# Decoder step on one core: cache tiles loaded from the Pool queue into three buffers, dilated queries kept in token order, one rotary table

## The chip, the cores and the metric

The kernel runs on one core of a Trainium2 chip. The metric is the device time of one execution in microseconds (us). A core has TensorE (PE; its weight loads are listed apart as PEld), VectorE (DVE), ScalarE (ACT), GpSimd (POOL) and SyncE (SP, which here only issues DMAs). Engines run their own instruction streams in order and meet through semaphores. "SPq" is the issuing side of SP.

## The reference, cut to what matters

Two layers of a decoder trunk are computed for 1024 prompt tokens and for a sample group of 8 sequences with 4 new tokens each. The first layer is gated linear attention, the second a dilated attention over one shared K/V. Both are followed by a SwiGLU and a gated embedding. What the change touches is the second layer's attention:

```python
DIL_GROUPS = ((128, 1), (512, 4), (2048, 16))
q = (h @ w_q).reshape(B, L, N_GROUPS, N_KV, Q_PER_KV, HEAD_DIM)   # 3 groups, 4 kv heads x 2, 128
q = rope_partial(rms_norm(q, q_norm), pos)
for g, (win, dil) in enumerate(DIL_GROUPS):
    o, l = attend(q[:, :, g], win, dil)     # prompt: a band of win/dil keys of the same class mod dil
    ...                                     # sample: the same keys, gathered from cache_k/cache_v + new ones
w = jax.nn.softmax(jnp.stack(lses), axis=0)
o = jnp.sum(w[..., None] * jnp.stack(outs), axis=0)
```

The sample tokens read `cache_k` and `cache_v`, of which the host lays out the 640 rows that any of the three groups can reach, per head and per half (four sequences) as five tiles of 128 x 512.

## The kernel before, in words

Tokens are columns: T = 1056 = 1024 prompt tokens (NP) and 32 sample tokens, cut into three chunks of CW = 352. Activations live as 128 x 1056 tiles, features on the partitions. Every large product is done as three products of rounded parts (`hi*hi`, `hi*lo`, `lo*hi`), each weight 128 x 128 against 352 columns. The program is traced in Python with a framework that sets all semaphores and that also sets the order on each engine's queue, from priorities and its own estimates of when things come due; a change of one operation can so move others.

The second layer's attention is the class `Mixer`, driven by `mixer`. There are eight head slots. For slot `s`, `queries(s)` makes three query tiles (one for each dilation group) from `XH`, `XL` (L949, 72 matmuls of 352 columns each tile), normalizes each with `qk_head` and turns the first 32 features by a rotary table. `attend(s, q)` then does the prompt attention, and after every second slot `sample(h, half)` is called twice for the sample tokens of that kv head. Products of the next slot's queries (L949) are woven between the small matmuls of `attend` and `sample`.

In `qk_head`, `finish` writes `q * g * rstd` into the query tile (L817). For the groups 1 and 2 (`classes=True`) it writes in class order instead: column `r*256 + u` holds token `4u + r` (L821), with a separate small instruction for the sample tokens of the last chunk (L825). The rotary table for those two groups is a second one in class order (`c_rope[1]`). `rotate` (L829 to L832) is the same for all. `sample_part` copies the sample columns of each query tile to `Qs` on POOL (L956).

In `attend`, group 0 is matched against `KA` (keys in token order, L985); the groups 1 and 2 against `KB` (the same keys in class order, copied by POOL at L933), with the queries of class `r` and half `h` as the stationary operand (L996): a contiguous run of 128 columns. Each of these matmuls is issued as two passes with a weight load each. The keys are 128 columns wide for `h = 0` and 256 for `h = 1`.

In `sample`, five key tiles `kk` (128 x 512, L1091) and five value tiles `vv` (L1136) are loaded by SP into two buffers each; eight small matmuls read each tile (L1095, L1139), after which its buffer is free. SP also issues, in the same queue, the query weights (`raw`, L260), `KA`, `VB`, `VA` (L931 to L939), the small round trips through DRAM for softmax statistics (`scr`, `stX`, `cA`, L989 to L1019) and the results.

Of the kernel before, what the change touches and what calls it, by code (L numbers as in the profile page):

```python
# [19 lines left out]
T = NP + NS  # L20
# [15 lines left out]
def yoco_step_kernel(  # L36
# [768 lines left out]
    def qk_head(chunks, g, tab, tp, dst, pre, late, classes=False, early=False):  # L805
# [4 lines left out]
        def finish(s, q, t, th, tl):  # L810
            p = sm.pools[0].tile([128, CW], F32, tag="sm", name="p_n")
            nc.tensor.matmul(p, ones_r, th, start=True, stop=False)
            nc.tensor.matmul(p, ones_r, tl, start=False, stop=True)
            nc.scalar.activation(t, p, AF.Ln, scale=1.0 / 128, bias=epsb)
            nc.scalar.activation(t, t, AF.Exp, scale=-0.5)
            if not classes:
                nc.vector.scalar_tensor_tensor(dst[:, s], q, g, t, op0=ALU.mult, op1=ALU.mult)  # L817
                return
            e = min(s.stop, NP) - s.start
            u = slice(s.start // 4, (s.start + e) // 4)  # L820
            nc.vector.scalar_tensor_tensor(  # L821
                dst[:, :NP].rearrange("p (r u) -> p u r", r=4)[:, u], q[:, :e].rearrange("p (u r) -> p u r", r=4), g,
                t[:, :e].rearrange("p (u r) -> p u r", r=4), op0=ALU.mult, op1=ALU.mult)
            if e < CW:
                nc.vector.scalar_tensor_tensor(dst[:, NP:], q[:, e:], g, t[:, e:], op0=ALU.mult, op1=ALU.mult)  # L825
# [23 lines left out]
    def rope_table(pool, i=0):  # L849
        tab = pool.tile([64, T], F32, name=f"tab{i}")  # L850
        nc.sync.dma_start(tab, c_rope[i])
# [46 lines left out]
    class Mixer:  # L898
        def __init__(self, st, mq):
# [14 lines left out]
            self.tab = [rope_table(p, i) for i in range(2)]  # L914
# [37 lines left out]
        def queries(self, s):  # L952
# [7 lines left out]
            for g in range(3):  # L960
                q = self.pool.tile([128, T], F32, tag="q", name="q", bufs=QB)
                flush = qk_head(self.proj(wtile(w_q[3 * s + g]), XH, XL), gcol(G_Q), self.tab[g > 0], self.pool, q,
                                self.pre, late, classes=g > 0)
# [5 lines left out]
        def attend(self, slot, q):  # L969
# [20 lines left out]
            for r in range(4):  # L990
                for h in range(2):
                    n = 128 * (h + 1)
                    s = slice(r * 256 + 128 * h, r * 256 + 128 * h + 128)
# [87 lines left out]
        def sample(self, h, half):  # L1081
# [8 lines left out]
            for a in range(5):  # L1090
                kk = sp.tile([128, 512], F32, tag="kk", name="kk", bufs=2)  # L1091
                nc.sync.dma_start(kk, ck[h, half, a])
# [42 lines left out]
            for a in range(5):  # L1135
                vv = sp.tile([128, 512], F32, tag="vv", name="vv", bufs=2)  # L1136
                nc.sync.dma_start(vv, cv[h, half, a])
# [211 lines left out]
```

## Time and profile before

| | us |
|---|---|
| median of three runs | 2946.8 (2945.55 to 2947.34) |
| the profiled execution, whole | 2945.02 |
| its span, first to last instruction | 2943.2 |
| TensorE busy in the span | 2891.9 (98%) |
| VectorE / ScalarE / GpSimd busy | 1851.8 / 1087.5 / 19.8 |
| mean granted TensorE clock | 0.996 |

The two feed-forward blocks keep TensorE busy without a break. The attention of the second layer lies between about 1440 and 2060 us of the span. The profile gives for each engine its busy time, for each group of instructions a count, busy time and mean, and for idle time what ended it.

### The profile page before, as it was taken

How to read it: one execution, taken by the hardware profiler on the slowest of the kernel's cores; microseconds unless marked ns; L12 is line 12 of the kernel's file. 1: busy time of each engine (PE TensorE's matmuls, PEld its weight loads, DVE VectorE, ACT ScalarE, POOL GpSimd, SP SyncE). 2: the span in 40 equal slices, each digit the busy share in tenths (PEclk: the TensorE clock that was granted, in tenths of full speed). 3: DMA queues.
4: the chain of work that ended last, by engine and by line, in shares of the span. 5: the costliest groups of instructions: out<-in, count | busy, mean ns of one | idle time of the engine just before them, and what ended most of it. 6: DMA issues, size and time to landing. Idle time of an engine off the chain costs nothing.

```text
span 2943.2 us, 47238 instructions
## 1 busy us (share of the span) xinstructions
PE 2891.9 (98%) x19920; PEld 2757.5 (94%) x19920; DVE 1851.8 (63%) x2781; ACT 1087.5 (37%) x1769; POOL 19.8 (1%) x44
## 2 busy tenths in 40 slices
PE   8999999999999999999999999989999999999999
PEld 7999898999999999999988888878899999999999
DVE  6444465776666544568587778774676666653474
ACT  5333344422222221235455555552532222231141
POOL 0000000000000000000000000000000000000000
PEclk9999999999999999999999999999999999999999
DMA  3121244222222532142523141334422222262123
GB/s 130 59 74 51 74 145 162 105 88 73 81 82 72 198 115 67 47 141 88 152 73 109 52 124 44 116 116 133 162 81 73 88 73 81 77 235 77 51 80 111
DMA packets 134419, 291.07 MB, mean 99 GB/s; under 512 B 34592, under 2 KB 59168, under 8 KB 133184
## 3 DMA queue, kind: packets, MB, share of 16 engines
q1 hardware_dynamic: 133040, 287.72, 29.7%
q8 instruction: 157, 2.57, 0.4%
q10 hardware_dynamic: 1168, 0.34, 0.1%
q14 instruction: 54, 0.44, 0.0%
HBM read 216.15 MB, written 71.86 MB: 98 GB/s over the span
## 4 chain that ended last, share of the span: by engine, by line
PE 89%; DVE 5%; DMA 3%; ACT 2%; issue 1%; SPq 0%; DVEq 0%; ACTq 0%
PE mm L271 39%; PE be L207 13%; PE ga L207 9%; PE al L207 9%; PE mm L949 6%; PE mm L681 2%; PE p_s L996 1%; PE mm L289 1%; DMA vv<-in_cv_dram 1%; PE p_o L1064 1%; PE p_s L985 1%; DVE q L821 1%; DVE hs L829 1%; PE p_u L505 1%; PE p_o L514 1%
## 5 line engine op out<-in xcount | busy, mean ns | idle before, releaser
L134 ACT CAST whi<-raw 128x1024 fp32r<-128x1024 f32 (+2 forms) x244 | 197.6, 810 | 774.6 <-PE mm L271 562.0
L776 DVE TENSOR_TENSOR X<-mm,X 128x1056 f32<-128x1056 f32 (+1 forms) x100 | 120.8, 1212 | 238.2 <-PE mm L271 238.1
L135 DVE TENSOR_TENSOR wlo<-raw,whi 128x1024 fp32r<-128x1024 f32 (+2 forms) x244 | 224.3, 919 | 72.0 <-ACT whi L134 71.9
L271 PE MATMUL mm<-XH,whi 128*128 128x352 f32 x1104 | 250.8, 331 | 0.4 <-ACT q_in L295 0.4
L271 PE MATMUL mm<-XH,wlo 128*128 128x352 f32 x1104 | 247.2, 328 | 0.0
L271 PE MATMUL mm<-XL,whi 128*128 128x352 f32 x1104 | 244.9, 326 | 0.0
L134 ACT CAST hw<-S 128x512 fp32r<-128x512 f32 x176 | 108.9, 621 | 313.3 <-PE ga L207 181.6
L271 PE MATMUL mm<-GH,wlo 128*128 128x352 f32 x1038 | 223.5, 323 | 0.0
L271 PE MATMUL mm<-GL,whi 128*128 128x352 f32 x1038 | 223.5, 323 | 0.0
L271 PE MATMUL mm<-GH,whi 128*128 128x352 f32 x1038 | 223.1, 323 | 0.0
L207 PE MATMUL be<-Bh,hw 128*128 128x264 f32 x1056 | 215.9, 286 | 5.2 <-ACT hw L134 5.2
L207 PE MATMUL be<-Bl,hw 128*128 128x264 f32 x1056 | 215.0, 285 | 0.0
L207 PE MATMUL be<-Bh,lw 128*128 128x264 f32 x1056 | 214.3, 284 | 0.0
L271 PEld LDWEIGHTS mm<-XH,whi 128*128 128x128 f32 x1104 | 188.8, 189 | 7.6 <-ACT XH L137 1.7
L949 PE MATMUL mm<-XH,whi 128*128 128x352 f32 x576 | 193.9, 337 | 0.0
L949 PE MATMUL mm<-XL,whi 128*128 128x352 f32 x576 | 193.9, 337 | 0.0
L271 PEld LDWEIGHTS mm<-XL,whi 128*128 128x128 f32 x1104 | 189.5, 189 | 3.4 <-issue 2.7
L271 PEld LDWEIGHTS mm<-XH,wlo 128*128 128x128 f32 x1104 | 189.1, 189 | 2.7 <-issue 2.0
L949 PE MATMUL mm<-XH,wlo 128*128 128x352 f32 x576 | 189.6, 329 | 0.0
L271 PEld LDWEIGHTS mm<-GL,whi 128*128 128x128 f32 x1038 | 177.0, 188 | 0.3 <-DVE GL L135 0.2
L271 PEld LDWEIGHTS mm<-GH,whi 128*128 128x128 f32 x1038 | 176.5, 188 | 0.0
L271 PEld LDWEIGHTS mm<-GH,wlo 128*128 128x128 f32 x1038 | 176.5, 189 | 0.0
(346 smaller groups left out, 6281.8 us busy)
## 6 DMA issues: line engine op xcount, KB each, us to landing
raw<-in_w_fi_dram SPq DMA_DIRECT2D x88, 512.0 KB, 3.5
Gd<-g SPq DMA_DIRECT2D x44, 528.0 KB, 2.7
gr<-Gd SPq DMA_DIRECT2D x44, 528.0 KB, 4.9
raw<-in_w_fo_dram SPq DMA_DIRECT2D x64, 256.0 KB, 2.7
raw<-in_w_a_dram SPq DMA_DIRECT2D x24, 512.0 KB, 3.5
raw<-in_w_q_dram SPq DMA_DIRECT2D x24, 512.0 KB, 3.6
kk<-in_ck_dram SPq DMA_DIRECT2D x40, 256.0 KB, 3.1
vv<-in_cv_dram SPq DMA_DIRECT2D x40, 256.0 KB, 3.0
```

The source lines that it names most:

```text
L134: nc.scalar.copy(hi, x)
L135: nc.vector.tensor_tensor(lo, x, hi.bitcast(F32), op=ALU.subtract)
L207: nc.tensor.matmul(ps[:, c, :HC], a[:, k, :], b[:, c * HC:(c + 1) * HC], start=(first and k == 0 and i == 0), stop=(k == len(xs) - 1 and i ...
L271: nc.tensor.matmul(ps[:, c, :CW], a[:, k, :], b[k][:, c * CW:(c + 1) * CW], start=(k == 0 and i == 0), stop=(k == n - 1 and i == 2),)
L289: nc.tensor.matmul(ps, a[:, k, :], b[k][:, s], start=(k == 0 and i == 0), stop=(k == n - 1 and i == 2))
L505: nc.tensor.matmul(p, kr[:, j], vt[:, j], start=True, stop=True)
L514: nc.tensor.matmul(po[:, i], vt[:, j, v], atts[j // 4][:, j % 4], start=True, stop=(j == 0))
L681: nc.tensor.matmul(ps[:, c, :CW], raw[:, 128 * k:128 * k + 128], ps_[k][:, c * CW:(c + 1) * CW], start=(k == 0), stop=(k == 1))
L776: nc.vector.tensor_tensor(like(X[m], s, p), p, like(X[m], s, p), op=ALU.add)
L821: nc.vector.scalar_tensor_tensor(dst[:, :NP].rearrange("p (r u) -> p u r", r=4)[:, u], q[:, :e].rearrange("p (u r) -> p u r", r=4), g, t[: ...
L829: nc.vector.stream_shuffle(t[32:64], dst[:32], [(a + 16) % 32 for a in range(32)])
L949: nc.tensor.matmul(ps, a[:, k, :], b[k][:, s], start=(k == 0 and i == 0), stop=(k == n - 1 and i == 2))
```

## The change

There are three edits. The query tiles of the groups 1 and 2 are written in token order like those of group 0, so `qk_head` loses its `classes` branch (L819 to L825) and the mixer its second rotary table; `attend` then takes the queries of a class as every fourth column of the query tile (L993). The key and value cache tiles are loaded by a DMA issued from the POOL queue. Each of the two has three buffers.

```diff
--- before.py
+++ after.py
@@ -802,7 +802,7 @@
         return tc.keep_in_program_order(nc.scalar.preload_act_table_set("natural_log_exp_and_others"))
 
 
-    def qk_head(chunks, g, tab, tp, dst, pre, late, classes=False, early=False):
+    def qk_head(chunks, g, tab, tp, dst, pre, late, early=False):
         def flush():
             while late:
                 late.pop(0)()
@@ -813,16 +813,7 @@
             nc.tensor.matmul(p, ones_r, tl, start=False, stop=True)
             nc.scalar.activation(t, p, AF.Ln, scale=1.0 / 128, bias=epsb)
             nc.scalar.activation(t, t, AF.Exp, scale=-0.5)
-            if not classes:
-                nc.vector.scalar_tensor_tensor(dst[:, s], q, g, t, op0=ALU.mult, op1=ALU.mult)
-                return
-            e = min(s.stop, NP) - s.start
-            u = slice(s.start // 4, (s.start + e) // 4)
-            nc.vector.scalar_tensor_tensor(
-                dst[:, :NP].rearrange("p (r u) -> p u r", r=4)[:, u], q[:, :e].rearrange("p (u r) -> p u r", r=4), g,
-                t[:, :e].rearrange("p (u r) -> p u r", r=4), op0=ALU.mult, op1=ALU.mult)
-            if e < CW:
-                nc.vector.scalar_tensor_tensor(dst[:, NP:], q[:, e:], g, t[:, e:], op0=ALU.mult, op1=ALU.mult)
+            nc.vector.scalar_tensor_tensor(dst[:, s], q, g, t, op0=ALU.mult, op1=ALU.mult)
 
         def rotate():
             t = tp.tile([64, T], F32, tag="hs", name="hs")
@@ -846,9 +837,9 @@
         late.append(rotate)
         return flush
 
-    def rope_table(pool, i=0):
-        tab = pool.tile([64, T], F32, name=f"tab{i}")
-        nc.sync.dma_start(tab, c_rope[i])
+    def rope_table(pool):
+        tab = pool.tile([64, T], F32, name="tab")
+        nc.sync.dma_start(tab, c_rope[0])
         return tab
 
 
@@ -911,7 +902,7 @@
             self.Qs = [p.tile([128, 8, 32], F32, name=f"Qs{h}") for h in range(4)]
             self.kn = p.tile([128, 4, 32], F32, name="kn")
             self.os = p.tile([128, 8, 8, 4], F32, name="os")
-            self.tab = [rope_table(p, i) for i in range(2)]
+            self.tab = rope_table(p)
             self.head(0)
             self.pre = ln_exp_set()
             for h in range(4):
@@ -959,8 +950,8 @@
 
             for g in range(3):
                 q = self.pool.tile([128, T], F32, tag="q", name="q", bufs=QB)
-                flush = qk_head(self.proj(wtile(w_q[3 * s + g]), XH, XL), gcol(G_Q), self.tab[g > 0], self.pool, q,
-                                self.pre, late, classes=g > 0)
+                flush = qk_head(self.proj(wtile(w_q[3 * s + g]), XH, XL), gcol(G_Q), self.tab, self.pool, q,
+                                self.pre, late)
                 late.append(lambda g=g, q=q: sample_part(g, q))
                 out.append(q)
             flush()
@@ -990,7 +981,7 @@
             for r in range(4):
                 for h in range(2):
                     n = 128 * (h + 1)
-                    s = slice(r * 256 + 128 * h, r * 256 + 128 * h + 128)
+                    s = slice(512 * h + r, 512 * h + 512, 4)
                     ps = sc.tile([128, 2 * n], F32, tag="sc", name="p_s")
                     for g in range(2):
                         nc.tensor.matmul(ps[:, g * n:g * n + n], q[1 + g][:, s], self.KB[:, r * 256:r * 256 + n],
@@ -1088,8 +1079,8 @@
             s0 = sc.tile([128, 512], F32, tag="sc", name="p_ss")
             s1 = sc.tile([128, 144], F32, tag="sc", name="p_ss")
             for a in range(5):
-                kk = sp.tile([128, 512], F32, tag="kk", name="kk", bufs=2)
-                nc.sync.dma_start(kk, ck[h, half, a])
+                kk = sp.tile([128, 512], F32, tag="kk", name="kk", bufs=3)
+                nc.gpsimd.dma_start(kk, ck[h, half, a])
                 out = s0[:, a * 128:(a + 1) * 128] if a < 4 else s1[:, :128]
                 for q, b, rs in quads():
                     nc.tensor.matmul(out[rs], Qs[:, b], kk[:, q * 128:(q + 1) * 128], start=True, stop=True,
@@ -1133,8 +1124,8 @@
             nc.scalar.copy(pt[:16, 5], p[:16, 1])
             po = self.po.tile([128, 128], F32, tag="sm", name="p_os")
             for a in range(5):
-                vv = sp.tile([128, 512], F32, tag="vv", name="vv", bufs=2)
-                nc.sync.dma_start(vv, cv[h, half, a])
+                vv = sp.tile([128, 512], F32, tag="vv", name="vv", bufs=3)
+                nc.gpsimd.dma_start(vv, cv[h, half, a])
                 for q, b, rs in quads():
                     nc.tensor.matmul(po[rs], pt[:, a, rs], vv[:, q * 128:(q + 1) * 128], start=(a == 0), stop=False,
                                      tile_position=(0, 32 * q))
```

## Rows read from the trace of the kernel before

**Rows 1.** The page's part 1: busy us (share of span) xinstructions of each engine.
```profile
PE 2891.9 (98%) x19920; PEld 2757.5 (94%) x19920; DVE 1851.8 (63%) x2781; ACT 1087.5 (37%) x1769; POOL 19.8 (1%) x44
```

**Rows 2.** Busy us by window: length, PE, PEld, DVE, ACT, POOL, PEclk, DMA share, GB/s.
```profile
1440.00:2060.00 620.00, 591.41 (x4043) 523.64 (x4042) 456.63 (x1100) 319.91 (x745) 17.08 (x32) 0.99 0.33 98
600.00:700.00 100.00, 100.00 (x821) 100.00 (x820) 68.86 (x94) 28.05 (x40) 0.00 (x0) 1.00 0.24 80
1600.00:1610.00 10.00, 8.21 (x81) 6.98 (x80) 8.33 (x22) 4.14 (x11) 0.72 (x1) 0.89 0.70 241
1610.00:1620.00 10.00, 9.47 (x78) 7.80 (x78) 4.45 (x9) 3.70 (x9) 0.00 (x0) 0.94 0.35 104
```

**Rows 3.** Waits of PE, 1440 to 2060 us: who for whom, total, times, longest.
```profile
PE p_os L1139 <- DMA vv<-in_cv_dram: 4.6, 7, 1.8
PE p_s L985 <- DVE stA L978: 3.1, 7, 0.9
PE mm L949 <- DVE OL L135: 3.0, 2, 2.7
PE p_t L1053 <- DVE pA L1050: 2.9, 3, 1.8
PE p_ss L1095 <- DMA kk<-in_ck_dram: 2.7, 4, 1.3
```

**Rows 4.** Timeline of SP's issues from 1600 us: start, us, what.
```profile
1600.61 1.18 SPq L1137 DMA_DIRECT2D vv<-in_cv_dram  x2
...
1606.89 5.69 SPq L1137 DMA_DIRECT2D vv<-in_cv_dram  x3
```

**Rows 5.** Timeline of PE from 1606 us: start, us, what, idle time before and releaser.
```profile
1606.40 0.43 PE L1139 MATMUL p_os<-vv,pts 128*32 128x128 f32 x8 [1.79 <-DMA vv<-in_cv_dram]
...
1608.57 0.49 PE L949 MATMUL mm<-XL,whi 128*128 128x352 f32 x1
```

**Rows 6.** DMA issues, 1440 to 2060 us: what, engine, count, KB each, median us to landing.
```profile
kk<-in_ck_dram SPq DMA_DIRECT2D x40, 256.0 KB, 3.1
vv<-in_cv_dram SPq DMA_DIRECT2D x40, 256.0 KB, 3.0
```

**Rows 7.** DVE by line and shape, 1440 to 2060 us: count, busy us, mean ns, idle before.
```profile
L821 DVE SCALAR_TENSOR_TENSOR q<-hq,gt,ht 128x352 f32<-128x352 f32 x32 | 27.4, 856 | 6.3 <-ACT ht L815 6.3
L817 DVE SCALAR_TENSOR_TENSOR q<-hq,gt,ht 128x352 f32<-128x352 f32 x24 | 13.7, 575 | 2.0 <-ACT ht L815 2.0
L821 DVE SCALAR_TENSOR_TENSOR q<-hq,gt,ht 128x320 f32<-128x320 f32 x16 | 12.7, 793 | 8.5 <-ACT ht L815 8.5
L825 DVE SCALAR_TENSOR_TENSOR q<-hq,gt,ht 128x32 f32<-128x32 f32 x16 | 3.6, 228 | 0.0
```

**Rows 8.** PE by line and shape, 1470 to 2060 us, the same columns.
```profile
L996 PE MATMUL p_s<-KB,q 128*128 128x256 f32 x128 | 36.7, 399 | 0.6 <-DVE stA L978 0.5
L996 PE MATMUL p_s<-KB,q 128*128 128x128 f32 x128 | 22.4, 288 | 0.5
```

**Rows 9.** Timeline of PE in three short stretches, as in Rows 5.
```profile
1507.14 0.33 PE L949 MATMUL mm<-XH,whi 128*128 128x352 f32 x1
1507.31 0.32 PE L949 MATMUL mm<-XL,whi 128*128 128x352 f32 x1
...
1511.59 0.50 PE L996 MATMUL p_s<-KB,q 128*128 128x128 f32 x3
...
1512.31 0.81 PE L996 MATMUL p_s<-KB,q 128*128 128x256 f32 x3
```

**Rows 10.** ACT by line and shape, 1470 to 2060 us, as in Rows 7.
```profile
L1042 ACT COPY o<-p_o 128x512 f32<-128x512 f32 x16 | 17.4, 1089 | 1.6 <-PE p_o L1040 1.1
L1128 ACT COPY pts<-p_ts 128x512 f32<-128x512 f32 x8 | 4.7, 586 | 11.2 <-PE p_ts L1127 11.2
```

**Rows 11.** POOL by line and shape, 1440 to 2060 us, as in Rows 7.
```profile
L933 POOL COPY KB<-KA 128x1024 f32<-128x1024 f32 x4 | 8.1, 2035 | 28.3 <-issue 22.4 <-DMA KA<-Kd 6.0
L956 POOL COPY Qs<-q 128x32 f32<-128x32 f32 x24 | 7.9, 328 | 460.1 <-DVE q L832 401.1 <-DVE ls L1119 59.0
```

## The prediction, made before the changed kernel was run

> **What bounds the kernel now.** I read the windows first. In the feed-forward blocks TensorE has no idle time, and the change touches nothing there; from 1440 to 2060 us, where the edited code runs, it is busy 591.4 of 620 us [rows 1]. So TensorE is the bound, and only its idle time and what it does can move the end. The idle time is 28.6 us, a ceiling for all that shorter waits can bring. In the same stretch DVE is busy 456.6 us and POOL 17.1 us. Then the waits of TensorE there, by what ended them [rows 2]: 4.6 us for value tiles (vv) and 2.7 us for key tiles (kk), so 7.3 us in 11 waits for the cache; 3.1, 3.0 and 2.9 us for DVE. Last, the queue behind the longest cache wait: SP issues two vv tiles at 1600.6 us, TensorE stands 1.79 us until 1606.4 us for one of them, and only then do three more go out, over 5.7 us, since each needs a buffer that TensorE has first read empty [rows 3, 4]. [...]
>
> **Part 1, cache tiles from the POOL queue, three buffers.** Removed: 80 issues from SP's queue with their waits for a free buffer. SP's other issues (query weights, KA, VA, VB, the statistics) no longer stand behind these. No wait of TensorE for query weights is among the rows, so this alone is put at nothing; a query weight is split long before its matmuls. Gain: at most the 7.3 us [rows 2], and nothing if the tiles come no sooner. With three buffers three of the five tiles of a half are there ahead of time instead of two, and the last two still wait for a buffer; I take 5 us. The low clock costs (1 - 0.89) x 10 + (1 - 0.94) x 10 = 1.7 us [rows 1]; it follows the 1.79 us wait, and if that is only shortened the clock may still fall, so 1 us of it (bounds 0 and 1.7). Added: 80 issues on POOL. No row shows a DMA issued by POOL. Its cost there is bounded by nothing from below, since POOL is idle for 603 of 620 us [rows 1], and by POOL's dearest instruction, 2.035 us [rows 5], from above: 80 x 2.035 = 163 us, still hidden. What stands behind a waiting issue on POOL are the Qs copies (L956) and the KB copies (L933). The Qs copies of a head come before the small matmuls that free that head's buffers, and a KB copy serves the next head, so I put nothing. A tile that comes later by POOL than by SP (3.0 and 3.1 us to landing now [rows 6]) is the third rival.
>
> **Part 2, queries in token order on DVE.** Today 32 scattered writes of 352 columns take 856 ns, 16 of 320 columns 793 ns and 16 small ones 228 ns; the plain write of 352 columns takes 575 ns [rows 7]. So 32 x (856 - 575) = 9.0 us and 16 x (793 + 228 - 575) = 7.1 us, together 16.1 us off an engine that is not the bound. On the path lies only what TensorE waits for DVE: 9.0 us in the three rows [rows 2], the upper bound; the lower is nothing. DVE loses 16.1 / 456.6 = 3.5% of its work there, and in the last slot, where no query products are left to fill in, 0.28 + 0.45 = 0.7 us come straight off the queue ahead of the last queries. I take 1.5 us. What is late next is the rotation (L829 to L832), which stays.
>
> **Part 3, one rotary table.** One load of 264 KB less at the start of the stage. TensorE waits for no table in the rows: nothing. Its space pays for the buffers.
>
> **Part 4, weight loads with a step of four.** This is the price. There are 256 passes of L996 in the eight slots, half with 128 columns, half with 256 [rows 8], each with a weight load of 128 columns from the query tile, which now takes every fourth float, one in each 16 bytes. The load for a pass runs under the pass before it, so it costs what exceeds that cover. The starts tell the cover: passes of 128 columns follow each other at (0.50 - 0.275) / 2 = 0.11 us, those of 256 at (0.81 - 0.38) / 2 = 0.215 us (three starts, and the length of one pass, 275 or 379 ns) [rows 9, 10]; products of 352 columns at about 0.16 us [rows 4]. A contiguous load thus takes 0.11 us at most. In every class four passes of 128 columns and then four of 256 are issued: 96 loads (3 x 8 slots x 4 classes) lie behind a 128-column pass of their own run, 96 behind a 256-column pass, and 64 at the heads of runs, mostly behind a product. No row shows TensorE reading with a step. Faster than contiguous is excluded: the same 128 columns are read. Lower bound: nothing, if the load still fits under 0.11 us. Nearest row for the other side: ScalarE copies 512 columns in 586 ns, and in 1089 ns where it writes every fourth float (L1042) [rows 11], so 0.98 ns more for each element; 128 x 0.98 = 0.126 us, a load of 0.236 us: 96 x 0.126 + 96 x 0.02 + 64 x 0.076 = 18.9 us. I take a load twice as long, 0.21 us, because the ScalarE pair is nearly a doubling (1089 / 586 = 1.86): 96 x 0.10 + 96 x 0 + 64 x 0.05 = 12.8 us. TensorE has no idle time beside these passes to swallow it (0.6 and 0.5 us before all of them [rows 8]), so it counts in full.
>
> [...]
>
> **The sum.** 2945.0 (the profiled execution) - 5 - 1 - 1.5 + 12.8 = 2950.3 us. The median of the runs is 1.8 us above the profiled execution, so 2952 us, 5 us or 0.18% above before. Its own range: with 18.9 us and a gain of only 3 us, 2963; with 12.8 us and all of the bounds of the gains, 7.3 + 1.7 + 9.0 = 18 us, 2942.
>
> **Rivals.** *The step is free.* The load stays hidden under 0.11 us and only the gains are left: 2946.8 - 7.5 = 2939 us, between 2929 (all 18 us) and 2944 (3 us). For it: a contiguous load need not fill its 0.11 us. Against it: the only rows with this step show it at nearly half rate. It decides at 0.11 us for a load. [...]
>
> *The step is dearer.* At 0.236 us for a load part 4 is 18.9 us and the kernel 2946.8 - 7.5 + 18.9 = 2958 us. It decides at 0.215 us, from where the 256-column passes are no full cover any more.
>
> *POOL's tiles come later.* A ring of two buffers with 3.05 us from issue to landing brings 2 / 3.05 = 0.66 tiles a us; with three buffers it brings the same at 4.6 us. If POOL's issue takes 1.6 us longer than SP's, the 5 + 1 us don't come, and at 0.5 us more than that the 11 waits may grow by some 0.2 us each, 2 us. With the 12.8 us of the step: 2946.8 + 12.8 - 1.5 + 2 = 2960 us, slower than before; with a free step 2947. For it: the transfers of 1600 to 1610 us share DMA engines that are 0.70 busy [rows 1], so to issue earlier may only be to queue earlier. Against it: only 7.3 us of waits for 80 tiles; most come in time. [...]
>
> *It doesn't do what it says.* The order on TensorE's queue is made afresh from the framework's estimates, so a wait may only move. That is in the ranges.
>
> **How the numbers follow.** The step at about twice a load, with the gains: 0.45. The step free: 0.3. The step dearer: 0.1. POOL's tiles later, with a step that costs: 0.15. Faster and slower mean by more than 0.2%, 5.9 us, about what a measurement of this kernel tells from no change. Faster is 0.8 of the free step and a little of the likeliest case: 0.26. Slower is 0.36 of the likeliest case, whose middle lies just under the bound, and nearly all of the two dear cases: 0.38. The same: 0.36. The time is the likeliest case's, 2952 us, own range 2942 to 2963. The range for 8 in 10 takes in the middle of the free step and of the dear ones: 2937 to 2961 us.
>
> **What would show it.** The spacing of L996 passes of 128 columns: 0.11 us if the step is free, 0.21 if it is as I say, over 0.23 if dearer, and then over 0.215 for 256 columns too. The waits of TensorE for vv and kk: under 3 us if part 1 works, 7 or more if POOL is late; POOL's us to landing, under or over 4.6. L821 and L825 gone and all 72 writes at about 575 ns. The granted clock around the first sample part at 1.0 if its wait is gone. I am wrong if L996 stays at 0.11 us, if waits of TensorE for the Qs or KB copies turn up, or if the stage's idle time moves by more than the 18 us of all bounds.

## The result, and the profile after

| | before | after |
|---|---|---|
| median of four runs, us | 2946.96 (2945.55 to 2947.34) | 2961.83 (2961.23 to 2968.47) |
| ratio, 95% interval | | 1.0059 (1.0045 to 1.0073) |
| the profiled execution and its span, us | 2945.02, 2943.2 | 2968.47, 2966.7 |
| stage, us | 596.7 | 619.3 |
| TensorE idle in the stage, us | 27.1 | 34.1 |
| granted clock at 0.50 in the stage, us | 10.2 | 37.5 |

The changed kernel is slower, by 14.9 us between the medians and 17 by the ratio; measured a second time it took 2963.9 us, 1.0068 (1.0053 to 1.0083) times the kernel before there, which is 20 us. "Stage" is the time from the first to the last of the query and output products (L949 before, L940 after: behind the edit of the query write, line numbers are 9 lower). The span is 23.5 us longer in the profiled execution and the stage 22.6, so the loss lies where the edited code runs. Of the 22.6 us, 7.0 are idle time of TensorE (13.4 more in waits for cache tiles, 6.4 less in all others) and 15.6 are work that takes it longer. (This execution was the longest of the four; the profiled one of the second measurement has a stage of 616.1 us.)

The numbers in [rows n] are those of the groups above. The prediction's pointers are off in places: where it names rows 1, 2, 3 and 4, 5, 9 and 10, and 11, it reads Rows 2, 3, 4 and 5, 11, 9, and 10; the spacing of products of 352 columns, for which Part 4 names rows 4, is in Rows 9, too.

Windows of the kernel after (us, busy us of PE, PEld, DVE, ACT, POOL, granted clock, DMA share, GB/s), beside [rows 2]:

```profile
1610.00:1620.00 10.00, 10.00 (x74) 8.16 (x67) 5.42 (x7) 1.26 (x4) 2.80 (x6) 0.66 0.24 64
1740.00:1745.00 5.00, 5.00 (x58) 4.37 (x58) 2.27 (x12) 1.93 (x5) 1.59 (x3) 1.00 0.75 240
1745.00:1750.00 5.00, 1.39 (x12) 0.72 (x12) 2.57 (x9) 1.99 (x5) 0.00 (x0) 0.74 0.60 226
1750.00:1755.00 5.00, 5.00 (x24) 3.87 (x24) 1.03 (x3) 0.27 (x1) 1.07 (x2) 0.50 0.33 107
```

A wait that was 1.79 us long has become waits of over 3.5 us, in which TensorE works 1.39 of 5 us, and after one the granted clock stands at 0.50 for a whole window of 5 us. Waits of PE in the kernel after, 1440 to 2060 us (who for whom, total us, times, longest), beside [rows 3]:

```profile
PE p_os L1130 <- DMA vv<-in_cv_dram: 14.6, 8, 3.7
PE p_ss L1086 <- DMA kk<-in_ck_dram: 6.1, 11, 1.4
PE mm L940 <- DVE OL L135: 2.4, 1, 2.4
PE p_t L1023 <- DVE pB L1021: 2.1, 3, 0.7
```

The waits for cache tiles are 20.7 us, not under 7.3. Those for DVE have shrunk: over all rows they are 5.7 us of the stage where they were 11.8. Then the place of one long wait. POOL's issues and PE's matmuls in the kernel after (start, us, what, count, idle time before and its releaser), beside [rows 4, 5]:

```profile
1742.92 1.59 POOL L1128 DMA_DIRECT2D vv<-in_cv_dram  x3 [3.19 <-PE p_os L1130]
1750.05 0.54 POOL L1128 DMA_DIRECT2D vv<-in_cv_dram  x1 [5.55 <-PE p_os L1130]
```
```profile
1742.16 0.86 PE L1130 MATMUL p_os<-vv,pts 128*32 128x128 f32 x24
...
1745.14 0.32 PE L940 MATMUL mm<-XH,whi 128*128 128x352 f32 x1
1749.07 0.65 PE L1130 MATMUL p_os<-vv,pts 128*32 128x128 f32 x8 [3.61 <-DMA vv<-in_cv_dram]
...
1750.41 0.49 PE L940 MATMUL mm<-XH,whi 128*128 128x352 f32 x1
```

PE takes the three tiles that are there in one run of 24 matmuls. Only when the first of them is used up can POOL issue the next three; PE has other work for 2.5 us and then stands 3.61 us for the fourth tile of the half. Behind the wait a product takes 0.49 us instead of 0.32. All but 0.1 of the 14.6 us for vv fall on a half's fourth tile. The transfers in the kernel after, 1440 to 2060 us (count, KB, median us to landing), beside [rows 6]:

```profile
kk<-in_ck_dram POOLq DMA_DIRECT2D x40, 256.0 KB, 3.7
vv<-in_cv_dram POOLq DMA_DIRECT2D x40, 256.0 KB, 3.7
```

Last the edited instructions of the kernel after (count, busy us, mean ns, idle before), beside [rows 7, 8, 11]: three of POOL, DVE's query write, PE's score passes over KB and their weight loads.

```profile
L1083 POOL DMA_DIRECT2D kk<-in_ck_dram x40 | 22.0, 553 | 54.4 <-PE p_ss L1086 47.6 <-DMA kk<-in_ck_dram 5.6 <-PE p_ss L1089 1.0
L1128 POOL DMA_DIRECT2D vv<-in_cv_dram x40 | 21.3, 536 | 77.4 <-PE p_os L1130 57.3 <-DMA vv<-in_cv_dram 19.9 <-issue 0.3
L924 POOL COPY KB<-KA 128x1024 f32<-128x1024 f32 x4 | 9.1, 2277 | 27.3 <-issue 26.8 <-DMA KA<-Kd 0.5
```
```profile
L816 DVE SCALAR_TENSOR_TENSOR q<-hq,gt,ht 128x352 f32<-128x352 f32 x72 | 43.4, 603 | 22.9 <-ACT ht L815 22.0
```
```profile
L987 PEld LDWEIGHTS p_s<-KB,q 128*128 128x128 f32 x256 | 64.3, 327 | 1.2 <-DVE stA L969 0.5
L987 PE MATMUL p_s<-KB,q 128*128 128x256 f32 x128 | 39.7, 423 | 0.3 <-DVE stA L969 0.3
L987 PE MATMUL p_s<-KB,q 128*128 128x128 f32 x128 | 33.6, 375 | 0.0
```

### The profile page after: what moved, and what is told of

It is laid out like the page before. It is cut to its first block, busy times and chain, and to the rows that moved or that the text cites. A ratio compares the mean times of both kernels' runs of the same rounds, so it can differ in the third digit from the quotient of the medians.

```text
span 2966.7 us, 47288 instructions
## 1 busy us (share of the span) xinstructions
PE 2909.7 (98%) x19920; PEld 2792.2 (94%) x19920; DVE 1844.5 (62%) x2765; ACT 1086.5 (37%) x1769; POOL 63.0 (2%) x124
## 4 chain that ended last, share of the span: by engine, by line
PE 88%; DMA 4%; DVE 3%; issue 3%; ACT 2%; POOL 0%; SPq 0%; POOLq 0%; ACTq 0%
PE mm L271 39%; PE be L207 13%; PE ga L207 9%; PE al L207 8%; PE mm L940 6%; PE mm L681 2%; PE p_s L987 1%; DMA vv<-in_cv_dram 1%; PE mm L289 1%; DMA kk<-in_ck_dram 1%; PE p_o L1055 1%; PE p_s L976 1%; PE p_u L505 1%; PE p_o L514 1%; PE p_t L306 1%
## 5 line engine op out<-in xcount | busy, mean ns | idle before, releaser
L271 PE MATMUL mm<-XH,wlo 128*128 128x352 f32 x1104 | 247.8, 329 | 0.0
L940 PE MATMUL mm<-XH,wlo 128*128 128x352 f32 x576 | 195.0, 339 | 0.0
L940 PE MATMUL mm<-XL,whi 128*128 128x352 f32 x576 | 193.6, 336 | 0.0
L940 PE MATMUL mm<-XH,whi 128*128 128x352 f32 x576 | 192.8, 335 | 0.0
```

The source lines that it names most:

```text
L271: nc.tensor.matmul(ps[:, c, :CW], a[:, k, :], b[k][:, c * CW:(c + 1) * CW], start=(k == 0 and i == 0), stop=(k == n - 1 and i == 2),)
L940: nc.tensor.matmul(ps, a[:, k, :], b[k][:, s], start=(k == 0 and i == 0), stop=(k == n - 1 and i == 2))
```

## The experiments

Each ratio is against runs of the kernel before on the same chip. "Waits" is what PE waited for vv and kk from 1440 to 2060 us in the profiled execution.

| kernel | queue, buffers, how a pass reads its queries | median us | ratio (95%) | stage us | waits us |
|---|---|---|---|---|---|
| before | SP, 2, adjacent | 2946.96 | 1 | 596.7 | 7.3 |
| e2_step_only | SP, 2, step 4 | 2946.03 | 1.0014 (1.0004 to 1.0023) | 598.3 | 6.7 |
| e3_sp3 | SP, 3, step 4 | 2942.06 | 1.0004 (0.9994 to 1.0013) | 593.8 | 5.8 |
| e4_pool2_class | POOL, 2, adjacent | 2942.97 | 1.0007 (0.9997 to 1.0016) | 598.4 | 12.6 |
| e1_after_contig | POOL, 3, adjacent | 2945.59 | 1.0010 (1.0000 to 1.0019) | 604.9 | 20.5 |
| r_after | POOL, 3, step 4 | 2963.9 | 1.0068 (1.0053 to 1.0083) | 616.1 | 20.2 |
| e5_sp3_contig | SP, 3, adjacent | 2931.45 | 0.9961 (0.9950 to 0.9972) | 582.8 | 6.9 |
| e6_class1_sp3 | SP, 3, adjacent (class) | 2942.2 | 0.9999 (0.9990 to 1.0009) | 594.4 | 5.3 |
| e7_pool_vv | vv POOL, kk SP, 3, step 4 | 2959.07 | 1.0056 (1.0041 to 1.0071) | 609.1 | 16.4 |
| e8_pool2_step | POOL, 2, step 4 | 2967.53 | 1.0082 (1.0067 to 1.0097) | 619.8 | 24.0 |
| e9_poolcopy | SP, 2, adjacent (copied) | 2955.19 | 1.0039 (1.0024 to 1.0054) | 606.9 | 5.5 |
| e10_sp3_step2 | SP, 3, step 2 | 2927.23, one run | | 579.9 | 5.2 |
| e11_pool_kk | kk POOL, vv SP, 3, step 4 | 2950.42 | 1.0022 (1.0012 to 1.0032) | 605.0 | 15.4 |
| e12_bulk_pool | POOL with the large transfers, 3, step 4 | 2952.43 | 1.0036 (1.0023 to 1.0049) | 603.6 | 13.4 |
| e13_half_sp3 | SP, 3, step 2 | 2927.36 | 0.9950 (0.9935 to 0.9965) | 577.7 | 2.1 |

### One half of the change at a time

**e1_after_contig**, the kernel after with

```diff
-                    s = slice(512 * h + r, 512 * h + 512, 4)
+                    s = slice(512 * h + 128 * r, 512 * h + 128 * r + 128)
```

> The changed kernel with the weight loads of L987 taken from 128 neighbouring columns instead of every fourth; the scores of the groups 1 and 2 are then of the wrong queries, the work is the same, and every engine's queue has the same order. Theory A, the step is the whole loss: passes of 128 columns 0.11 us apart again, 18 us less than the changed kernel, about 2944 us. Theory B, the step is half hidden and the waits for cache tiles from POOL are the other half: about 2953 us, waits of TensorE for vv and kk still near 20 us in a profile.

1.0010. The time is near theory A's, and the waits of 20.5 us are theory B's. Its runs lie between 2940.8 and 2955.6 us and the profile is of the longest. All instructions stand in the same order as after. The stage is 14.4 us shorter than that of the kernel after, which has the same 37.5 us at a granted clock of 0.50, and 11.2 shorter than in r_after (the kernel after measured again), which has 27.3: that is the step's.

**e2_step_only**, the kernel after with SP's queue and two buffers again:

```diff
-                kk = sp.tile([128, 512], F32, tag="kk", name="kk", bufs=3)
-                nc.gpsimd.dma_start(kk, ck[h, half, a])
+                kk = sp.tile([128, 512], F32, tag="kk", name="kk", bufs=2)
+                nc.sync.dma_start(kk, ck[h, half, a])
...
```

The vv load is edited likewise.

> The kernel before with token order, the step of four and one table; the cache tiles stay on SP with two buffers. Theory A: 2947 + 18 - 1.5 = about 2963 us. Theory B: 2947 + 9 - 1.5 = about 2954 us, waits of TensorE for the cache near the 7 us of before.

1.0014, about 4 us. Both theories were off. The passes over KB follow each other 0.234 us apart here too, at either width, and all of them take 60.8 us of PE's time where before they took 48.5. But PE's idle time in the stage fell from 27.1 to 18.8 us with the same queue and buffers, and its waits for DVE from 11.8 to 4.8: DVE's saving gives most of the price back.

**e3_sp3**, the kernel after with `nc.sync` at both loads.

> The changed kernel with its cache tiles issued by SP, still three buffers, step of four. Theory A, the issuing queue does not matter: 2961 us, and waits for vv and kk as in the changed kernel. Theory B, POOL's tiles come later and its order bunches the small matmuls: waits for vv and kk under 7 us, about 2953 us.

1.0004, level, with waits of 5.8 us as theory B had them and a time below both theories'. With the step's price in full, the third buffer and DVE's saving pay for it. So POOL's queue is the other half of the loss.

**e4_pool2_class**, the kernel before with `nc.gpsimd` at both loads.

> The kernel before with its cache tiles issued by POOL, two buffers, class order and both tables kept. Theory A: 2945 to 2947 us, no change. Theory B: waits of TensorE for the cache over 12 us and 2953 us or more.

1.0007: in class order with two buffers POOL costs little, though the waits rise from 7.3 to 12.6 us.

### Both halves on one chip, and their sum

**r_after** is the kernel after again, and **e5_sp3_contig** is e3_sp3 with the slice of e1_after_contig.

> The changed kernel itself, on the chip of the next three runs. The experiments so far were timed on another chip than the changed kernel was, so what it loses there isn't settled. Theory C (the step costs 12 to 13 us of PE's passes, DVE's relief gives most of that back, and the waits and low clock behind POOL's issues cost some 15 us more): 15 to 20 us over the kernel before. Rival (the loss of the first measurement was that chip's; both halves are small, as the one-sided kernels of the first batch say): within 6 us of the kernel before.

> The changed kernel with SP issuing the cache tiles (three buffers kept) and with the dilated queries read as 128 adjacent columns, so each score pass computes other queries' scores than the reference's. Theory C: nothing of the loss is left and both gains stand, DVE's relief of about 10 us and the third buffer's 4: 12 to 16 us under the kernel before. Rival (the passes with the step run beside waits that exist anyway, and contiguous reading only lets these waits show): 0 to 5 us under the kernel before, as the kernel with SP, three buffers and the step was level with it.

1.0068 and 0.9961, both as theory C said or near it. The four kernels with three buffers and token order form a square (e1 and e3 ran on one chip, r_after and e5 on another):

| stage, us | adjacent | step 4 | difference |
|---|---|---|---|
| SP | 582.8 | 593.8 | 11.0 |
| POOL | 604.9 | 616.1 | 11.2 |
| difference | 22.1 | 22.3 | |

That the two prices add almost to a tenth is luck: the profile of e1_after_contig is 10 us above that kernel's median, with 37.5 us at a granted clock of 0.50 where r_after has 27.3, e5_sp3_contig 10.2 and e3_sp3 6.8. The ratios take in all runs. By them the step is 0.43% on SP's queue and 0.58% on POOL's (12.7 and 17 us), and POOL 0.49% and 0.64% (14 and 19 us). The passes of e5_sp3_contig, to be read beside those of after above (loads, passes of 256 and of 128 columns):

```profile
L987 PEld LDWEIGHTS p_s<-KB,q 128*128 128x128 f32 x256 | 41.7, 194 | 6.1 <-DVE stB L969 2.8 <-DVE stA L969 0.8
L987 PE MATMUL p_s<-KB,q 128*128 128x256 f32 x128 | 35.8, 392 | 0.8 <-DVE stA L969 0.4 <-DVE stB L969 0.3
L987 PE MATMUL p_s<-KB,q 128*128 128x128 f32 x128 | 21.6, 282 | 0.0
```

The loads differ: 194 ns each, and 327 with the step. (They overlap: 256 of them are busy for 41.7 and 64.3 us.)

### Which tiles, and which wait

**e7_pool_vv** and **e11_pool_kk** are the kernel after with `nc.sync` at the kk load alone, or at the vv load alone. **e8_pool2_step** is the kernel after with `bufs=2` at both.

> The changed kernel with only the vv tiles issued by POOL, and the kk tiles by SP. Theory C1 (the loss behind POOL is that of the vv tiles, which POOL issues in a bunch only when PE has released three: the waits of 3.6 us each, and the clock that falls behind them): the loss stays, 12 to 18 us over the kernel before, with vv's waits still near 14 us. Rival C2 (it is the kk tiles, which queue behind POOL's copy of the keys, and the vv issues that queue behind them): within 5 us of the kernel before, vv's waits back under 7 us.

> The changed kernel with only the kk tiles issued by POOL, and the vv tiles by SP. With the kernel that has only vv on POOL 16 us over the kernel before and both on POOL 20 over, theory C1 (vv's waits at the fourth tile, and the clock that falls behind them, are most of the loss) wants 2 to 6 us over the kernel before here. Rival (either kind on POOL costs the same, since one late queue is enough): 12 to 17 over.

> The changed kernel with two buffers for each kind of cache tile in place of three; POOL still issues them and the queries keep their step. What is asked: is it POOL's queue alone that costs the 15 us, or POOL's queue together with three buffers? With three buffers PE takes three tiles in one go and then wants the fourth, whose transfer starts only when the first of the three is used up; with two it takes two tiles and then one at a time. Theory D (queue and buffers together: all of PE's waits for vv stand at the fourth tile of five): 2 to 8 us over the kernel before, as the one-sided kernels with the step alone and POOL alone were 4 and 2 over. Rival (the queue by itself, as soon as the queries are in token order): 15 to 20 over.

vv on POOL costs 1.0056, kk 1.0022 (6.6 us, just over what was expected), both 1.0068, against 1.0004 with neither: mostly vv's, as theory C1 had it. But theory D falls. With two buffers the kernel is no better, 1.0082, and the waits have moved to kk. Waits of PE in e8_pool2_step:

```profile
PE p_ss L1086 <- DMA kk<-in_ck_dram: 18.6, 13, 3.6
PE p_os L1130 <- DMA vv<-in_cv_dram: 5.4, 6, 1.3
```

So the bunch of three was the shape that the loss took, not its cause. The place of the longest wait in e8_pool2_step shows more. First PE, then the transfers issued from 1597 to 1602 us (KB, median us to landing), then those from 1595.5 to 1596.6:

```profile
1605.92 0.65 PE L1086 MATMUL p_ss<-kk,Qs 128*32 128x128 f32 x8 [3.58 <-DMA kk<-in_ck_dram]
```
```profile
VA<-Vd SPq DMA_DIRECT2D x1, 512.0 KB, 4.9
Ad<-o SPq DMA_DIRECT2D x1, 512.0 KB, 5.6
kk<-in_ck_dram POOLq DMA_DIRECT2D x2, 256.0 KB, 6.3
```
```profile
kk<-in_ck_dram POOLq DMA_DIRECT2D x2, 256.0 KB, 3.0
```

The tile that PE stands for was issued at 1599.49 us, 1.8 us behind SP's load of VA and 1 us behind its store of o, and took over 6 us; the two before it took 3.0. Three heads have this wait behind VA and o: 3.58, 3.46 and 2.60 us. In e4_pool2_class a tile issued between the same two took 5.9 us as well, and PE had other work until it came.

The same pair of transfers stands ahead of vv in the long wait of the kernel after, and in e3_sp3, where the tiles follow it on SP's own queue. Transfers of the kernel after issued from 1740.5 to 1744.6 us, and of e3_sp3 from 1732.4 to 1737:

```profile
vv<-in_cv_dram POOLq DMA_DIRECT2D x3, 256.0 KB, 6.3
VA<-Vd SPq DMA_DIRECT2D x1, 512.0 KB, 6.6
Ad<-o SPq DMA_DIRECT2D x1, 512.0 KB, 7.1
```
```profile
vv<-in_cv_dram SPq DMA_DIRECT2D x3, 256.0 KB, 4.9
VA<-Vd SPq DMA_DIRECT2D x1, 512.0 KB, 4.3
Ad<-o SPq DMA_DIRECT2D x1, 512.0 KB, 4.9
```

In this head each of the five takes 1.4 to 2.3 us longer where two queues issue them; in r_after, the same kernel as after, the same five took 4.8, 5.3 and 4.5 to 4.8 us, no longer than in e3_sp3. One place does not settle it. Over the stage I took for each of the 80 tiles the time from issue to landing, and called it "beside" where a query weight, KA, VB, VA or the store of o was in transit on SP's queue for over 1 us of it:

| | tiles beside, mean us | PE's wait for them, us | tiles alone, mean us | PE's wait for them, us |
|---|---|---|---|---|
| before | 43, 3.90 | 4.9 | 37, 2.88 | 2.4 |
| e3_sp3 | 33, 4.04 | 3.6 | 47, 3.24 | 2.2 |
| r_after | 44, 4.86 | 16.9 | 36, 3.26 | 3.3 |
| e8_pool2_step | 45, 4.62 | 18.8 | 35, 2.96 | 5.3 |

Alone, a tile lands as soon from POOL's queue as from SP's (3.26 against 3.24 us with three buffers, 2.96 against 2.88 with two). Beside a large transfer it takes 0.7 to 0.8 us longer from POOL's at the same number of buffers, and nearly all of the added wait falls there.

**e12_bulk_pool** puts the large transfers into POOL's queue too: the kernel after with `nc.gpsimd` at the loads of KA, VB and VA and at the store of o.

> The changed kernel with the large transfers of the attention (KA, VB and VA of a head, and the store of o) issued by POOL too, so that they stand in one queue with the cache tiles again, as they did in SP's. Theory E (a cache tile on POOL's queue shares the 16 DMA engines with a large transfer that SP has under way: in the trace of the changed kernel tiles take 4.9 us beside one and 3.3 alone, and 17 of the 21 us of PE's waits for tiles fall on the former): tiles beside large transfers fall to about 4 us, PE's waits for tiles to 6 to 12 us, and the time to 4 to 12 us over the kernel before. Rival (POOL's queue is late by itself, 0.27 us more from release to issue and 0.2 us more an issue, whatever stands on SP's): the waits stay near 20 us and the time 17 to 24 over.

1.0036, 10 us over before instead of 20. Waits of PE:

```profile
PE p_os L1130 <- DMA vv<-in_cv_dram: 8.6, 8, 2.1
PE p_ss L1086 <- DMA kk<-in_ck_dram: 4.8, 8, 1.2
```

13.4 us, a little more than theory E wanted, and far from the rival's 20. But the tiles don't land as theory E has it. The same five transfers in e12_bulk_pool, all from one queue again, issued from 1735.5 to 1739.5 us:

```profile
vv<-in_cv_dram POOLq DMA_DIRECT2D x3, 256.0 KB, 6.4
VA<-Vd POOLq DMA_DIRECT2D x1, 512.0 KB, 5.4
Ad<-o POOLq DMA_DIRECT2D x1, 512.0 KB, 5.7
```

Over the stage, the 27 tiles beside a large transfer of POOL's own queue take 4.71 us in e12_bulk_pool, hardly less than the 4.86 of r_after; the 25 beside a query weight on SP take 4.06. What did change is the order on PE's queue, which the framework sets. PE at this place, first in e3_sp3, then in e12_bulk_pool, to be read beside its 3.61 us in the kernel after:

```profile
1739.22 0.43 PE L1130 MATMUL p_os<-vv,pts 128*32 128x128 f32 x8 [0.49 <-DMA vv<-in_cv_dram]
```
```profile
1744.09 0.43 PE L1130 MATMUL p_os<-vv,pts 128*32 128x128 f32 x8 [2.12 <-DMA vv<-in_cv_dram]
```

The three heads that have this place (VA, o, then three vv tiles, the first of them the fourth of its half); "cover" is the time from the issue of that fourth tile until PE has nothing else to do, and the count is of PE's matmuls between the third tile and the fourth:

| | VA and o by, vv by | vv tiles, us to landing | matmuls | cover, us | PE's wait for the fourth, us |
|---|---|---|---|---|---|
| e3_sp3 | SP, SP | 4.5 to 5.4 | 23 | 4.3 | 0.56, 0.49, 0.93 |
| e11_pool_kk | SP, SP | 4.7 to 6.7 | 23 | 4.3 | 2.17, 0.54, 1.14 |
| after | SP, POOL | 6.0 to 6.4 | 14 | 2.5 | 3.67, 3.61, 3.55 |
| r_after | SP, POOL | 4.5 to 6.2 | 14 | 2.5 to 2.6 | 3.25, 1.97, 3.47 |
| e7_pool_vv | SP, POOL | 5.4 to 5.9 | 14 | 2.5 | 2.87, 3.15, 3.02 |
| e12_bulk_pool | POOL, POOL | 5.4 to 6.5 | 24 | 4.1 | 1.88, 2.12, 1.26 |

From POOL's one queue the tiles land no sooner than from two, and from SP's one queue they took up to 6.7 us too. But in the kernel after PE comes for the fourth tile 2.5 us after its issue, not 4.1 to 4.3, so that the same landing makes it wait longer. Of the 6.9 us by which the waits of e12_bulk_pool lie under r_after's, 3.4 are at these three tiles, which land later in e12_bulk_pool, and 4.3 at kk's (4.8 us against 9.1, but 6.1 in the profile of the kernel after); the other vv tiles have 0.8 more. So theory E isn't shown. Half of POOL's price goes when POOL issues the large transfers too, and PE's order is a part of that; quicker transfers behind VA and o are not. The other half, 9 us against e3_sp3, stays open; 7.6 us of it in the profiled stages are waits for tiles. What the trace shows of it: POOL issues 0.33 us after the end of PE's last matmul on the buffer where SP does 0.06 us after it, an issue lasts 0.54 us on POOL and 0.33 to 0.37 on SP (medians), and the clock is low for 17 us of the stage against 7.

### Versions that might beat both

**e6_class1_sp3**: the kernel before with three buffers, and one table in class order, which the near query reads through a view, each element 1 KB from the last.

```diff
+                nc.vector.tensor_tensor(o[:, :NP].rearrange("p (u r) -> p u r", r=4), x[:, :NP].rearrange("p (u r) -> p u r", r=4), tab[a:b, :NP].rearrange("p (r u) -> p u r", r=4), op=ALU.mult)
...
```

> A version that could beat both: the kernel before with three buffers, SP issuing, queries kept in class order, and only the one table in class order, which the near query reads with a step. DVE keeps the two strided writes and has two strided reads with a tail more for each near query, 8 in all. Theory C: the third buffer's 4 us less DVE's added reads (16 instructions a little longer and 16 tails, 2 to 4 us of DVE, a part of it on the path): 0 to 4 us under the kernel before. Rival (DVE's strided reads cost what strided writes do, 50 per cent more): 2 us over to 1 under.

0.9999. Against e5_sp3_contig, which has the same queue, buffers and adjacent reading, DVE does 24.5 us more (1864.7 against 1840.2), and the kernel is 10.8 us slower. DVE's scattered reads are dear, as the rival had it: 1998 ns for 32x1024 where 32x1056 without a step takes 1246. Rows of e6_class1_sp3:

```profile
L832 DVE TENSOR_TENSOR q<-q,tab 32x1024 f32<-32x1024 f32 x8 | 16.0, 1998 | 0.1
...
L821 DVE SCALAR_TENSOR_TENSOR q<-hq,gt,ht 128x352 f32<-128x352 f32 x32 | 27.2, 851 | 5.7 <-ACT ht L815 5.7
```

**e9_poolcopy**: SP with two buffers; POOL copies each dilated query from token order into class order.

```diff
+                if g:
+                    late.append(lambda q=q, qt=qt: nc.gpsimd.tensor_copy(
+                        q[:, :NP].rearrange("p (r u) -> p r u", r=4), to_class(qt[:, :NP])))
...
```

> A version that could beat both: SP issues with two buffers, one table; the dilated queries are made in token order in a tile of their own, and POOL, which has little to do in this stage, copies each into class order (16 copies of 128x1024), so that the score passes read 128 adjacent columns. Theory (PE pays the step in full, DVE's relief stands, and a copy of 2.0 to 2.3 us on POOL lies beside other work): 11 to 13 us less than the kernel with the step alone, so 6 to 10 us under the kernel before. Rival (the score passes of the last query wait for POOL's copy, 2 us in each of 8 slots): 0 to 8 us over the kernel before.

1.0039, slower than even the rival's range. The copy takes 2168 ns, but the score passes wait for it, up to 6.6 us; waits of PE:

```profile
PE p_s L991 <- POOL q L957: 14.0, 8, 6.6
```

**e10_sp3_step2**: e3_sp3 with a step of two.

```diff
-                    s = slice(512 * h + r, 512 * h + 512, 4)
+                    s = slice(512 * h + 256 * (r // 2) + r % 2, 512 * h + 256 * (r // 2) + 256, 2)
```

> The kernel with SP, three buffers and the step, with a step of two columns (8 bytes) in place of four (16 bytes), so that it computes other queries' scores than the reference's. One look, for the spacing of the score passes over KB. If any step makes a weight load dear: 0.234 us for both shapes, and the time that the step of four gave. If the load's price goes by 16-byte lines: 0.11 us at 128 columns and 0.215 at 256, and some 11 us less.

2927.23 us in the one run, and the price is gone from the loads:

```profile
L987 PEld LDWEIGHTS p_s<-KB,q 128*128 128x128 f32 x256 | 42.6, 198 | 5.4 <-DVE stB L969 0.8 <-DVE stA L969 0.6
...
L987 PE MATMUL p_s<-KB,q 128*128 128x128 f32 x128 | 21.7, 282 | 0.0
```

A load with a step of 8 bytes takes 198 ns, as good as the 194 of adjacent columns.

**e13_half_sp3** makes use of that. It is the kernel before with three buffers and one table, with the dilated queries kept as even tokens, then odd tokens: a class is then every second column of one half.

```diff
-            u = slice(s.start // 4, (s.start + e) // 4)
+            v = slice(s.start // 2, (s.start + e) // 2)
             nc.vector.scalar_tensor_tensor(
-                dst[:, :NP].rearrange("p (r u) -> p u r", r=4)[:, u], q[:, :e].rearrange("p (u r) -> p u r", r=4), g,
+                dst[:, :NP].rearrange("p (k v) -> p k v", k=2)[:, :, v], q[:, :e].rearrange("p (v k) -> p k v", k=2), g,
...
-                    s = slice(r * 256 + 128 * h, r * 256 + 128 * h + 128)
+                    s = slice(512 * (r % 2) + 256 * h + r // 2, 512 * (r % 2) + 256 * h + 256, 2)
...
```

> A version that could beat both kernels: SP, three buffers, one table, and the dilated queries kept with the even tokens first and then the odd ones, so that DVE reads with a step of two and writes adjacent columns, and the score passes read with a step of two (8 bytes), which in the last look cost nothing (0.11 us at 128 columns). The one table stands in that order too, and the near query's rotation reads it through a view, with two tails of 32 columns. Theory F (the pass pays only for a step over 8 bytes, and DVE's write at step two lies nearer to the plain 603 ns than to the class write's 830): 8 to 16 us under the kernel before. Rival (DVE's write costs as much as the class write, and the relief is lost): 0 to 5 us under, as the class-ordered kernel with three buffers and one table was level.

0.9950 (0.9935 to 0.9965): 15 us under the kernel before and, by the ratios, some 32 to 35 us under the kernel after. DVE and the weight loads in e13_half_sp3:

```profile
L821 DVE SCALAR_TENSOR_TENSOR q<-hq,gt,ht 128x352 f32<-128x352 f32 x32 | 18.5, 578 | 5.4 <-ACT ht L815 5.4
...
L834 DVE TENSOR_TENSOR q<-q,tab 32x1024 f32<-32x1024 f32 x8 | 9.7, 1214 | 0.1
```
```profile
L1005 PEld LDWEIGHTS p_s<-KB,q 128*128 128x128 f32 x256 | 42.1, 200 | 8.2 <-DVE q L841 2.3 <-DVE stA L987 0.7 <-DVE stB L987 0.3
```

The write that took 856 ns takes 578, the near query's product with the table, now with the query read and written at a step of two, 1214 ns where the one with the scattered table took 1998, and the load 200. PE's waits for DVE in the stage are 4.8 us, against 11.6 in e6_class1_sp3.

## Why the prediction was wrong

The forecast was 2952 us with a range up to 2961, and 2961.8 was measured, so both the time and, barely, the range missed. The sum had one term with the wrong sign and one far too small, and the errors partly cancelled.

**Part 1 failed, and it is the step that decides.** The forecast was a gain of 5 us and 1 us of clock. The runs show a loss of about 14 to 19 us by the ratios: PE waits 20.7 us for cache tiles where it waited 7.3, and the granted clock is at 0.50 for 37.5 us of the stage where it was for 10.2. It split into two things that I had put into one line. Three buffers on SP's queue do bring something: e2_step_only to e3_sp3, 1.0014 to 1.0004, about 3 us, with intervals that overlap. The queue takes far more. I costed POOL's issues as hidden, rightly (they are 43 us on an idle engine), and moved on; two things I put at nothing. One is when the tiles land: beside SP's large transfers they took 4.9 us from POOL's queue (r_after) and 4.0 from SP's (e3_sp3). The other is PE's order, which I had noted as a rival and left "in the ranges": with vv on POOL, 14 matmuls lie ahead of the fourth tile, with vv on SP 23. The window of 1600 to 1610 us, where the DMA engines were 0.70 busy [rows 2], was in the text as a point for the third rival, and it was the right row for the first of the two.

**The third rival came about, at its time but not by its rule.** "POOL's tiles come later" gave 2960 us and had a chance of 0.15. It was to decide at a landing of 4.6 us, and the median landing is only 3.7. A median over tiles says little here: the 44 tiles beside SP's large transfers take 4.9 us in r_after, and three of these are tiles that PE wants next, with 8.7 of its 20.2 us of waits. The size was wrong too, 8 us for the lost gain and the added waits, where the queue alone cost 14 to 19; what it lacks is longer waits (13.4 us more, not 2) and the clock. Three of its six falls in the stage of the kernel after, 24 of the 37.5 us, stand at the three waits of 3.55 to 3.67 us. That its 2960 us lie so near to 2961.8 is luck: DVE's saving, put at 1.5 us, made up for most of what the queue cost beyond the 8.

The length of POOL's issues does not explain when its tiles land: a vv issue on POOL took 536 to 538 ns in every one of the nineteen from 1600 to 1760 us in r_after, and the tiles landed after 2.8 to 6.0 us.

**Part 4: the price was right and its make-up was not.** 12.8 us were forecast; on SP's queue the step costs 11.0 us in the stage and 12.7 by the ratios, on POOL's 17 by the ratios. But the load is no 0.21 us: passes follow each other every 0.234 us at 128 columns and 0.236 at 256, where before it was 0.112 and 0.216. That is the dearer rival's 0.236 almost to the nanosecond. At that length the forecast's own working gave 18.9, so that 12.8 came out is in part luck. It charged the 64 heads of runs 0.076 us each, and the time that PE's passes take, from the end of what ran before to their own, grew by only 12.0 us at 128 columns (15.0 to 27.0) and 3.0 at 256 (30.7 to 33.7), 15.0 in all against e5_sp3_contig; the stage grew by 11.0. Of these 4 us, 2.6 are idle time that e3_sp3 has less of (18.6 against 21.2), and its clock is low for 3.4 us less. The mark for "dearer" in the last part of the prediction was met.

The first rival, a free step, did not come about: the same 128 columns took 194 ns adjacent (e5_sp3_contig), 198 at a step of 8 bytes (e10_sp3_step2) and 327 at 16 (after). The price sets in between a step of two floats and a step of four; no run has a step of three.

**Part 2 was far too small.** 16.1 us less on DVE were forecast; the query writes fell from 57.4 us (the four rows of [rows 7]) to 43.4, so 14.0. On the path I took 1.5 us of it, from the argument that DVE is not the bound. e2_step_only is 4 us over before and carries a step worth 11 to 13, so DVE's saving gave back 7 to 9; e6_class1_sp3 and e13_half_sp3, which differ by 20.3 us of DVE's time (1864.7 to 1844.4) and in how a pass reads, differ by 0.49% or 14 us. The 9.0 us taken as the upper bound were only the three longest rows; all of PE's waits for DVE in the stage were 11.8 us, and 4.8 are left in e2_step_only, 5.7 in the kernel after. PE's idle time other than for tiles fell from 19.8 us to 13.4 (34.1 - 20.7). DVE, busy 456.6 of 620 us, was on the path more often than its share says, since it stands between one product and the next.

**Part 3** was tested by no run on its own; no wait of PE for a table is among the rows after either.

**The sum again**, with what the runs gave: step 11 to 13, DVE -7 to -9, third buffers -3, POOL 14 to 19. That makes 13 to 22 us; 17 and 20 were measured, by the ratios. As the terms are differences of the same runs, this only says that they fit together.

**What stays open**: the half of POOL's price that is left when it issues the large transfers too, why tiles land later from its queue beside a large transfer, and why two buffers on POOL cost 0.07% in class order and 0.82% in token order with a step. In class order PE waits 12.6 us for tiles and the clock is low for 6.8 us, in token order 24.0 and 23.9: the late tiles meet a busy PE in one and a waiting one in the other. No run kept PE's order and changed the queue alone.

## What to carry to other kernels

Before a stream of just-in-time tiles is moved to another DMA queue, look at two things: how long tiles take there beside large transfers (here 4.9 us in r_after, which the medians of 3.5 for vv and 3.8 for kk hide), and what work the engine that waits has between a tile's issue and its use. Where a framework sets the order, a change of queue can change that too (here 23 matmuls ahead of the fourth tile became 14), so count this work in both traces before a longer wait is put down to the transfers. A step of four floats in a weight load had a price here on the bound engine (327 ns a load against 194, and 11.0 us of the stage on SP's queue); a layout that splits it into two halves with a step of two was free for the load (200 ns) and for DVE's write (578 ns against 603 in token order). Cost a saving on a half-busy engine by all of the waits for it, not the longest rows alone, and expect a good part of them where it stands between two products: here 6 to 7 of 11.8 us went.

## What the hardware showed that was not expected

- A weight load of 128 columns of 128 rows took 194 ns from adjacent floats (e5_sp3_contig), 198 to 200 with a step of two (e10_sp3_step2, e13_half_sp3) and 326 to 327 with a step of four (e3_sp3, after, r_after); passes of 128 columns then follow each other after 0.11, 0.12 and 0.234 us.
- On DVE a product of 32x1024 with one operand read at jumps of 1 KB took 1998 ns (e6_class1_sp3), with one operand read and the result written at a step of two 1214 (e13_half_sp3), and 32x1056 without a step 1246 (e6_class1_sp3).
- Three transfers of 256 KB behind two of 512 KB landed after 4.5 to 5.4 us where SP issued all five (e3_sp3; 4.7 to 6.7 in e11_pool_kk), after 4.5 to 6.4 where POOL issued the three (after, r_after) and after 5.4 to 6.5 where POOL issued all (e12_bulk_pool).
- The issue of a cache tile took at its shortest 536 ns on POOL (r_after) and 327 ns on SP (e3_sp3); a tile beside no large transfer landed after 3.3 us from POOL's queue (r_after) and 3.2 from SP's (e3_sp3).
